# Norms of token tiles 4 to 7 written behind the turns of tiles 2 and 3, and the last product's weight difference written one product sooner

## The chip, the cores and the metric

One core of one Trainium2 chip runs the whole kernel. The metric is the device time of one execution in microseconds (us). Engines are named as in the profile: PE (TensorE matmul), PEld (its weight load), DVE (VectorE), ACT (ScalarE), POOL (GpSimd), SP (SyncE, which issues nearly all DMAs here).

## The reference

An encoder layer over 1024 tokens of width 1024, all in f32. In short:

```python
x = LN1(ALPHA * x + 0.5 * swiglu(x, ffn1_w1, ffn1_w3, ffn1_w2))     # width 2816 inside
...                                                                 # latent attention and S5 scan, merged
x = LN2(ALPHA * x + merged @ w_out)
x = LN3(ALPHA * x + 0.5 * swiglu(x, ffn2_w1, ffn2_w3, ffn2_w2))
x = LN4(ALPHA * x + sigmoid(x @ w_gate) * (p @ w_proj))
```

The change touches the two places where a SwiGLU ends in its layer norm (LN1 and LN3) and the next matmuls begin: the projection `w_u` of the S5 branch after LN1, the gate `ple_w_gate` after LN3.

## The kernel before, in words

**Precision.** Every f32 operand is split in two fp32r parts, high and low (`split`, L62: a copy on ACT, L64, and a subtraction on DVE, L65), and each product is three matmuls: high by high, high by low, low by high.

**The second layers** (`ffn_down`, L353) multiply the hidden activations by `w2` with Strassen's scheme (Winograd's form): seven products of half-sized blocks in the order 1, 5, 6, 3, 7, 2, 4, each over 11 slabs of the inner dimension, taken in six steps `q` (five pairs of slabs and a single one). Products alternate between two sets of four PSUM banks (`pd` and `pdy`). The weight blocks b11, b12, b21, b22 are fetched to SBUF and combined in place on DVE: `less` (L414) lists the products that take a difference, and L429 subtracts, step by step, just ahead of the splits of that step. Product 4, the last one, takes b21 - b11, written into b11's room. Its results complete token tiles 4 to 7 (128 tokens by 1024); tiles 0 to 3 are complete after product 2. `ffn_down` is a generator: it yields the tiles 0 to 3 with their row sums between the steps of product 4, and the tiles 4 to 7 one by one as their last addition (`add`, L392) is written.

**The norms** (`norm_in`, L187) consume these tiles. For each tile `layer_norm` (L113) is written: the mean on DVE (L120), the squares with a running sum on ACT (L123, into a scratch tile `scr`), a square root on ACT (L125), five small DVE operations (L126 to L130) and two passes over the tile on DVE (L133, L135). A normed tile is then *turned*: `transpose_in` (L139) has PE transpose it by eight 128x128 matmuls into a PSUM tile `tln` (L148), which is split into the transposed activations `xhi` (ACT, L64) and `xlo` (DVE, L65). The list `ready` holds normed tiles: with `lag=2` tile 0 is turned after norm 2 is written, tile 1 after norm 3, tile 2 after norm 4, tile 3 after norm 5. Tiles 4 to 7 are turned by `finish` (late turns, in half tiles), which the caller writes after the first half of the next matmuls.

**What follows.** After LN1: four splits of the `w_u` weights (`whi`, `wlo`), then `up` for tokens 0 to 511 (`pu`, 96 matmuls, whose moving operand is one row block of the transposed tiles 0 to 3, so all four must be turned), then `finish`, then `up` for tokens 512 to 1023. The S5 branch's parameters are loaded behind that. After LN3: `pgate` and `pproj` tile by tile (a gate tile j needs only turned tile j), each evacuated by a sigmoid on ACT (L1057, tile `gs`) and two DVE operations (L1058, L1061); `finish` is written between gate tile 3 and gate tile 4. There `scr` and `gs` are tiles of one tag with two buffers, and the transposed activations, the parameters of LN3 and those of LN4 are tiles of another tag (`x` of the pool `fb`) with three.

**The order on each engine** is not the order of writing. The kernel is built by a scheduler that reckons when each instruction's operands will be there; among those that it takes to be ready, the one written earlier goes first, and when none of the early ones is ready, a later one goes. Buffers of a tag are handed out as they are first written in that order. The engine then runs its list strictly in order. The caller's two lines are

```python
finish = norm_in(chain([first], dn), acc, *ln, x1T, fp, spill, 2)          # after LN1; spill stores a turned tile to DRAM
finish = norm_in(chain([first], dn), acc, gt, bt, x3T, fp, lag=2)          # after LN3
```

and LN2 uses the same function with `blocks=True`.

Of the kernel before, what the change touches and what calls it, by code (L numbers as in the profile page):

```python
# [45 lines left out]
def layer_kernel(ctx, tc, A):  # L46
# [68 lines left out]
    def layer_norm(a, sums, gt, bt, pool, out=None):  # L115

        nm, sq, v, y, rs = [sml.tile([128, 1], F32, tag=f"ln{i}", name=f"ln{i}") for i in range(5)]
        V.tensor_scalar(out=nm, in0=sums[:, 0:1], scalar1=sums[:, 1:2], scalar2=-1.0 / D,  # L120
                        op0=ALU.add, op1=ALU.mult)
        scratch = pool.tile([128, 1024], BF16, tag="s", bufs=2, name="scr")
        S.activation(scratch, a, AF.Square, bias=nm, accum_out=sq)  # L123
        V.tensor_scalar(out=v, in0=sq, scalar1=1.0 / D, scalar2=LN_EPS, op0=ALU.mult, op1=ALU.add)
        S.activation(sq, v, AF.Sqrt)  # L125
        V.reciprocal(y, sq)  # L126
        V.tensor_tensor(out=sq, in0=y, in1=y, op=ALU.mult)
        V.tensor_tensor(out=sq, in0=sq, in1=v, op=ALU.mult)
        V.tensor_scalar(out=sq, in0=sq, scalar1=-0.5, scalar2=1.5, op0=ALU.mult, op1=ALU.add)
        V.tensor_tensor(out=rs, in0=y, in1=sq, op=ALU.mult)  # L130
        cs = [slice(0, 1024)] if out is None else [slice(c, c + 512) for c in (0, 512)]
        for c in cs:
            V.scalar_tensor_tensor(out=a[:, c], in0=a[:, c], scalar=nm, in1=gt[:, c], op0=ALU.add, op1=ALU.mult)  # L133
        for c in cs:
            V.scalar_tensor_tensor(out=a[:, c], in0=a[:, c], scalar=rs, in1=bt[:, c], op0=ALU.mult, op1=ALU.add)  # L135
            if out is not None:
                nc.sync.dma_start(out[:, c], a[:, c])
# [49 lines left out]
    def norm_in(steps, acc, gt, bt, xT, pool, done=None, lag=3, blocks=False):  # L187


        ready = []  # L190

        def bring(late):
            j = ready.pop(0)
            if blocks:
                transpose_blocks(acc, j, xT)
            else:
                transpose_in(acc[j], j, xT, late)
            if done:
                done(j)

        def finish(n=8):
            while ready and n:
                bring(True)
                n -= 1

        for j, sums in steps:
            with ExitStack() as after:
                for i in behind_splits:
                    after.enter_context(tc.issue_after(i.ins))
                layer_norm(acc[j], sums, gt, bt, pool)  # L210
            ready.append(j)
            if len(ready) > lag and ready[0] < 4:
                bring(False)
        return finish
# [138 lines left out]
    def ffn_down(fp, acc, x0, hd, w2, homes, hs):  # L353

        W, ends = {}, {}
        sums = [sml.tile([128, 2], F32, tag="sums", bufs=8, name="sums") for _ in range(8)]

        def block(i, q):
            p, n = DUOS[q]
            t, o = (W[i], p) if p < 8 else (ends[i[0]], 3 * i[1] + p - 8)
            return t[:, o:o + n, :]

        def fetch(i):
            if i[0] not in ends:
                ends[i[0]] = homes["end", i[0]]("w2e", F32)
            W[i] = homes[i]("w2w", F32)
            for q in range(len(DUOS)):  # L370
                p, n = DUOS[q]
                behind(lambda: nc.sync.dma_start(block(i, q), w2[i[0], i[1]][:, p:p + n, :]))

        def behind(load):
            if hs:
                with tc.issue_after(hs[-1].ins):
                    load()
            else:
                load()

        X = [pdn.tile([128, 512], F32, tag="dn", name="pd") for _ in range(4)]
        follows = {1: 5, 5: 6, 6: 3, 3: 7, 7: 2, 2: 4}
        ahead = None

        def hload(i, q):
            n = DUOS[q][1] * 512
            return load_raw(hd[i - 1][q].rearrange("p a b -> p (a b)")[:, 0:n], n, hs)

        def add(out, j, n, ps, first, last):
            a = acc[j][:, n * 512:n * 512 + 512]  # L390
            if first or last:
                V.scalar_tensor_tensor(out=a, in0=a, scalar=ALPHA if first else 1.0, in1=ps, op0=ALU.mult, op1=ALU.add,  # L392
                                       accum_out=sums[j][:, n:n + 1] if last else None)
            else:
                V.tensor_tensor(out=a, in0=a, in1=ps, op=ALU.add)

        b11, b12, b21, b22 = (0, 0), (0, 1), (1, 0), (1, 1)

        stages = ((1, 0, True, [(0, 0, True, False)]), (5, 1, True, [(4, 1, True, False)]),
                  (6, 0, False, [(0, 1, True, False)]), (3, 1, False, [(0, 1, False, True)]),  # L400
                  (7, 0, False, [(4, 1, False, True)]), (2, 1, True, [(0, 0, False, True)]),
                  (4, 0, False, [(4, 0, True, True)]))
        want = {1: b11, 5: b12, 6: b22, 2: b21}
        right = {1: b11, 5: b11, 6: b11, 3: b22, 7: b12, 2: b21, 4: b11}
        less = {5: (b12, b11), 6: (b22, b11), 7: (b22, b12), 4: (b21, b11)}
        for i, bank, fresh, reads in stages:
            if i == 1:
                fetch(want[i])
            if bank == 1 and fresh:
                yy = [pup.tile([128, 1024], F32, tag="up", name="pdy") for _ in range(2)]  # L410
                Y = [t[:, c:c + 512] for t in yy for c in (0, 512)]
            P = Y if bank else X
            held = []
            for q, (p, n) in enumerate(DUOS):  # L414
                if q == 0:
                    h = ahead or hload(i, 0)
                else:
                    h = hload(i, q)
                if q == len(DUOS) - 1 and i != 4:
                    ahead = hload(follows[i], 0)  # L420
                if q == 2 and i != 4 and follows[i] in want:
                    fetch(want[follows[i]])
                if q == 4 and i in (1, 5):
                    for j in range(4):
                        behind(lambda: nc.sync.dma_start(acc[j + (i == 5) * 4], x0[j + (i == 5) * 4]))
                w = block(right[i], q)
                if i in less:
                    x, y = (block(b, q) for b in less[i])
                    V.tensor_tensor(out=w, in0=x, in1=y, op=ALU.subtract)  # L429
                hh, hl = [wts.tile([128, 1024], F32R, tag=t, name=o) for t, o in (("uh", "hh"), ("ul", "hl"))]  # L430
                wh, wl = [fp.tile([128, 1024], F32R, tag="v", bufs=4, name=o) for o in ("wh", "wl")]
                split(h[:, 0:n * 512], hh[:, 0:n * 512], hl[:, 0:n * 512])
                last = split(w, *[t[:, 0:n * 512].rearrange("p (a b) -> p a b", a=n) for t in (wh, wl)])
                held.append((p, n, hh, hl, wh, wl))
                if i == 4 and 0 < q < 5:
                    behind_splits[:] = last
                    yield q - 1, sums[q - 1]
                    behind_splits.clear()
                if i == 4 and q == 4:
                    continue  # L440

                def part(t, first_p=held[0][0]):
                    for p, n, hh, hl, wh, wl in held:
                        for a in range(n):
                            ts = slice(a * 512 + t * 128, a * 512 + t * 128 + 128)
                            ws = slice(a * 512, a * 512 + 512)
                            for m, (x, y) in enumerate(((hh, wh), (hh, wl), (hl, wh))):
                                PE.matmul(P[t], lhsT=x[:, ts], rhs=y[:, ws], start=(fresh and p + a == 0 and m == 0),  # L448
                                          stop=(p + a == NP - 1 and m == 2), skip_group_check=True)

                for t in range(4):
                    part(t)
                    if q == len(DUOS) - 1:
                        for j, nn, first, last in reads:
                            add(None, j + t, nn, P[t], first, last)
                        if i == 4:
                            yield 4 + t, sums[4 + t]
                held = []
# [1056 lines left out]
```

## Time and profile before

| | |
|---|---|
| median of 3 runs | 2328.61 us (2328.49 to 2328.64) |
| the profiled execution, its own time | 2328.71 us |
| its span, first to last instruction | 2326.8 us |
| mean granted TensorE clock, as a share of full speed | 0.992 |
| busy: PE, DVE, ACT, POOL | 2260.3, 1543.6, 971.1, 233.9 us |

The profile is one execution. The span leaves out 1.9 us of its own time. PE is busy nearly throughout, so the time is to be found in the few places where PE waits or runs at the lower of its two clock levels. A line of a timeline gives start, duration, engine, line, operation, what it writes and reads, and in brackets the idle time before it and what ended that. Durations of neighbours on one engine overlap a little; the step from one start to the next is what an instruction costs its engine.

### The profile page before, as it was taken

To read this page: it belongs to the slowest core of one execution; us is meant where nothing else is said; L and a number is where in the kernel's file an instruction comes from. 1 tells how busy PE (TensorE), PEld (TensorE's weight loads), DVE (VectorE), ACT (ScalarE), POOL (GpSimd) and SP (SyncE) were. 2 spreads that over 40 slices of the span, in tenths; PEclk is the share of its full clock that TensorE was granted. 3 is DMA by queue.
4 is the path that set the end of the run, shared out by engine and by line. 5 is a ranking of instruction groups with operands and counts; after the bars stand their busy time and mean duration, and the time that the engine had idled before them with its cause. 6 is when DMAs were issued, how large, how long until landed. Compare 5 with 4: busy or idle time off the path is not lost.

```text
span 2326.8 us, 28503 instructions
## 1 busy us (share of the span) xinstructions
PE 2260.3 (97%) x10784; PEld 1863.0 (80%) x10784; DVE 1543.6 (66%) x2437; ACT 971.1 (42%) x1419; POOL 233.9 (10%) x318
## 2 busy tenths in 40 slices
PE   9999999999989899989999999999999999999998
PEld 7888888877777788877888887788888888877776
DVE  7555555676565798947688885585655555755856
ACT  5333333333342344444478772234333333333626
POOL 0000000000003500002255452100000000000000
PEclk9999999999999999999999999999999999999999
DMA  4323333834244232326200115122323235633401
GB/s 158 113 87 118 96 108 97 305 137 157 92 146 146 82 109 85 103 84 256 72 10 19 37 73 218 36 100 77 118 91 114 91 122 196 243 138 112 140 10 73
DMA packets 104474, 265.63 MB, mean 114 GB/s; under 512 B 13328, under 2 KB 27920, under 8 KB 104336
## 3 DMA queue, kind: packets, MB, share of 16 engines
q1 hardware_dynamic: 104336, 263.80, 33.4%
q8 instruction: 85, 1.39, 0.2%
q14 instruction: 53, 0.43, 0.1%
HBM read 189.33 MB, written 74.42 MB: 113 GB/s over the span
## 4 chain that ended last, share of the span: by engine, by line
PE 47%; DVE 5%; ACT 2%; issue 1%; DMA 1%; SPq 0%; POOL 0%; DVEq 0%; ACTq 0%; POOLq 0%
PE px L240 9%; PE py L240 5%; PE pdy L448 4%; PE pd L86 4%; PE pd L448 3%; PE pgate L86 3%; PE ps L86 3%; PE pz L240 2%; PE pov L753 2%; PE tpp L740 2%; PE pya L86 2%; PE pyb L86 2%; PE pq L86 1%; PE pg L86 1%; PE pu L278 1%
## 5 line engine op out<-in xcount | busy, mean ns | idle before, releaser
L64 ACT ACTIVATE whi<-raw 128x1024 fp32r<-128x1024 f32 (+4 forms) x116 | 112.2, 974 | 189.6 <-PE pg L86 99.0
L65 DVE TENSOR_TENSOR wlo<-raw,whi 128x1024 fp32r<-128x1024 f32 (+4 forms) x116 | 137.7, 1192 | 62.8 <-ACT whi L64 60.4
L448 PE MATMUL pd<-wl,hh 128*128 128x512 f32 x352 | 139.6, 398 | 3.1 <-DVE wl L65 3.1
L86 PE MATMUL pg<-xlo,whi 128*128 128x512 f32 x352 | 138.8, 394 | 0.0
L86 PE MATMUL pg<-xhi,whi 128*128 128x512 f32 x352 | 138.7, 394 | 0.0
L448 PE MATMUL pd<-wh,hl 128*128 128x512 f32 x352 | 138.5, 394 | 0.0
L86 PE MATMUL pg<-xhi,wlo 128*128 128x512 f32 x352 | 138.3, 393 | 0.0
L64 ACT ACTIVATE wh<-w2w 128x1024 fp32r<-128x1024 f32 x56 | 59.3, 1059 | 174.3 <-PE pd L448 92.3
L448 PE MATMUL pd<-wh,hh 128*128 128x512 f32 x352 | 120.3, 397 | 1.3 <-ACT wh L64 1.3
L240 PE MATMUL py<-tch,fhl 128*128 128x512 f32 x320 | 106.0, 392 | 0.0
L448 PE MATMUL pdy<-wl,hh 128*128 128x512 f32 x264 | 104.4, 396 | 0.8 <-DVE wl L65 0.8
L448 PE MATMUL pdy<-wh,hl 128*128 128x512 f32 x264 | 104.2, 395 | 0.0
L65 DVE TENSOR_TENSOR hl<-raw,hh 128x1024 fp32r<-128x1024 f32 x84 | 94.6, 1132 | 9.1 <-ACT hh L64 9.1
L64 ACT ACTIVATE fhl<-raw 128x512 fp32r<-128x512 f32 x40 | 25.3, 633 | 179.9 <-PE px L240 177.3
L448 PE MATMUL pdy<-wh,hh 128*128 128x512 f32 x264 | 99.1, 395 | 0.0
L240 PE MATMUL px<-td,thi 128*128 128x512 f32 x320 | 98.8, 390 | 0.0
L65 DVE TENSOR_TENSOR pt<-tpp,pt 128x512 fp32r<-128x512 f32 x128 | 85.6, 685 | 11.6 <-ACT pt L64 10.3
L65 DVE TENSOR_TENSOR wl<-w2w,wh 128x1024 fp32r<-128x1024 f32 x56 | 68.5, 1223 | 33.8 <-ACT wh L64 33.8
L254 DVE TENSOR_TENSOR c<-raw 128x512 f32<-128x512 f32 x40 | 27.6, 689 | 93.9 <-PE px L240 93.9
L727 POOL TENSOR_SCALAR P<-P,sm 128x1024 f32<-128x1024 f32 x64 | 74.7, 1168 | 117.0 <-DVE sm L726 99.3
L86 PE MATMUL ps<-k,qh 96*128 96x512 f32 (+1 forms) x256 | 84.2, 407 | 1.9 <-ACT P L725 1.7
L448 PEld LDWEIGHTS pd<-wl,hh 128*128 128x128 f32 x352 | 66.2, 188 | 21.6 <-DVE wl L65 6.4
(433 smaller groups left out, 6274.1 us busy)
## 6 DMA issues: line engine op xcount, KB each, us to landing
raw<-in_ffn_w_dram SPq DMA_DIRECT2D x86, 512.0 KB, 3.7
raw<-hd SPq DMA_DIRECT2D x70, 512.0 KB, 3.3
hd<-c SPq DMA_DIRECT2D x88, 256.0 KB, 3.4
w2w<-in_ffn_w_dram SPq DMA_DIRECT2D x32, 512.0 KB, 6.4
hd<-s SPq DMA_DIRECT2D x60, 256.0 KB, 3.2
rawx<-in_xT_dram SPq DMA_DIRECT2D x16, 256.0 KB, 6.4
w2e<-in_ffn_w_dram SPq DMA_DIRECT2D x8, 512.0 KB, 8.0
acc<-in_x_dram SPq DMA_DIRECT2D x8, 512.0 KB, 6.2
```

The costliest lines, as they stand in the source:

```text
L64: a = S.activation(hi, src, AF.Copy)
L65: return a, V.tensor_tensor(out=lo, in0=src, in1=hi.bitcast(F32), op=ALU.subtract)
L86: PE.matmul(out, lhsT=a, rhs=b, start=(n == 0), stop=(n == last))
L240: PE.matmul(out, lhsT=x[:, ks], rhs=y[:, k, :], start=(first and n == 0), stop=(n == 11), skip_group_check=True)
L254: V.tensor_tensor(out=c[:, r], in0=r2[:, l], in1=r2[:, r], op=ALU.add)
L278: PE.matmul(o, lhsT=x[:, ks], rhs=b[y][:, k, :], start=(i == 0 and k == 0 and m == 0), stop=(i == 1 and k == 3 and m == 2), skip_group_che ...
L448: PE.matmul(P[t], lhsT=x[:, ts], rhs=y[:, ws], start=(fresh and p + a == 0 and m == 0), stop=(p + a == NP - 1 and m == 2), skip_group_chec ...
L727: G.tensor_scalar(out=P, in0=P, scalar1=sm, scalar2=1.0, op0=ALU.mult, op1=ALU.mult)
L740: PE.transpose(tp[:, k * 128:k * 128 + 128], P[:, (q * 4 + k) * 128:(q * 4 + k) * 128 + 128], idt)
L753: PE.matmul(p[:, 0:256], lhsT=vt[:, k, c0:c0 + 128], rhs=pt[k // 4][b][:, k % 4, :], start=(k == 0 and b == 0), stop=(k == 7 and b == 1))
```

## The change

Two edits. In `ffn_down` product 4 leaves the list `less`, and its subtraction is written in product 2 instead, step by step, behind the splits of b21. The operands, the result and its place are the same. In `norm_in`, when it isn't the form for LN2 (`blocks`), the tiles 4 to 7 are not normed as they come: they go to a list `left`, and if a normed tile waits to be turned, it is turned then (tile 2 when tile 4 comes, tile 3 when tile 5 comes, as before). Their norms are written in `finish`, all four ahead of the late turns.

```diff
-        ready = []
+        ready, left = [], []
...
         def finish(n=8):
+            while left:
+                j, sums = left.pop(0)
+                layer_norm(acc[j], sums, gt, bt, pool)
+                ready.append(j)
             while ready and n:
                 bring(True)
                 n -= 1
 
         for j, sums in steps:
+            if j > 3 and not blocks:
+                left.append((j, sums))
+                if ready:
+                    bring(False)
+                continue
             with ExitStack() as after:
...
-        less = {5: (b12, b11), 6: (b22, b11), 7: (b22, b12), 4: (b21, b11)}
+        less = {5: (b12, b11), 6: (b22, b11), 7: (b22, b12)}
...
                 held.append((p, n, hh, hl, wh, wl))
+                if i == 2:
+                    V.tensor_tensor(out=block(b11, q), in0=w, in1=block(b11, q), op=ALU.subtract)
```

## Rows read from the trace of the kernel before

**Rows 1.** The page's first part: busy time, share of span, instructions.

```profile
PE 2260.3 (97%) x10784; PEld 1863.0 (80%) x10784; DVE 1543.6 (66%) x2437; ACT 971.1 (42%) x1419; POOL 233.9 (10%) x318
```

**Rows 2.** Waits of PE: us in total, times, longest.

```profile
PE pu L86 <- DVE ln L124: 7.5, 2, 6.0
```

**Rows 3.** Stretches behind product 4, first SwiGLU: length, engines' busy time (instructions), clock, DMA.

```profile
663.90:672.10 8.20, 0.76 (x1) 0.29 (x1) 8.20 (x13) 6.83 (x12) 0.00 (x0) 0.68 0.64 205
672.10:677.00 4.90, 4.86 (x11) 3.80 (x12) 4.90 (x25) 0.41 (x2) 0.00 (x0) 0.50 0.05 20
677.00:696.30 19.30, 19.30 (x85) 15.81 (x84) 3.71 (x5) 1.09 (x2) 0.00 (x0) 1.00 0.34 137
```

**Rows 4.** Timeline of PE in that place.

```profile
661.99 1.91 PE L148 MATMUL tln<-idt,acc 128*128 128x128 f32 x16
669.85 0.76 PE L86 MATMUL pu<-xhi,whi 128*128 128x512 f32 x1 [5.95 <-DVE ln L124]
672.14 0.79 PE L86 MATMUL pu<-xlo,whi 128*128 128x512 f32 x1 [1.53 <-DVE ln L124]
```

**Rows 5.** Timeline of DVE in that place.

```profile
663.57 1.22 DVE L65 TENSOR_TENSOR wlo<-raw,whi 128x1024 fp32r<-128x1024 f32 x1
...
664.89 1.28 DVE L133 SCALAR_TENSOR_TENSOR acc<-acc,ln,ln 128x1024 f32<-128x1024 f32 x1
...
668.48 1.22 DVE L65 TENSOR_TENSOR xlo<-tln,xhi 128x1024 fp32r<-128x1024 f32 x1
...
669.67 1.28 DVE L133 SCALAR_TENSOR_TENSOR acc<-acc,ln,ln 128x1024 f32<-128x1024 f32 x1
670.87 1.22 DVE L65 TENSOR_TENSOR xlo<-tln,xhi 128x1024 fp32r<-128x1024 f32 x1
...
698.16 4.88 DVE L65 TENSOR_TENSOR xlo<-tln,xhi 128x512 fp32r<-128x512 f32 x8 [17.45 <-ACT xhi L64]
```

**Rows 6.** Timeline of ACT in that place.

```profile
662.22 1.13 ACT L123 ACTIVATE scr<-acc,ln 128x1024 bf16<-128x1024 f32 x1
...
663.35 1.99 ACT L64 ACTIVATE whi<-raw 128x1024 fp32r<-128x1024 f32 x2
665.25 1.00 ACT L64 ACTIVATE xhi<-tln 128x1024 fp32r<-128x1024 f32 x1
666.15 1.14 ACT L123 ACTIVATE scr<-acc,ln 128x1024 bf16<-128x1024 f32 x1
...
667.28 1.00 ACT L64 ACTIVATE xhi<-tln 128x1024 fp32r<-128x1024 f32 x1
```

**Rows 7.** Timeline of DVE: differences of product 4, during product 3.

```profile
554.17 1.22 DVE L429 TENSOR_TENSOR w2w<-w2w 128x1024 f32<-128x1024 f32 x1
...
562.19 1.82 DVE L429 TENSOR_TENSOR w2e<-w2e 128x1024 f32<-128x1024 f32 x2
```

**Rows 8.** Timeline of SP: first S5 parameter.

```profile
725.34 0.42 SPq L1095 DMA_DIRECT2D c_re<-in_c_re_dram  x1
```

**Rows 9.** Timeline of PE, second SwiGLU: late turns.

```profile
2226.00 1.91 PE L148 MATMUL tln<-idt,acc 128*128 128x128 f32 x16
```

**Rows 10.** Timeline of DVE in that place.

```profile
2215.71 4.88 DVE L135 SCALAR_TENSOR_TENSOR acc<-acc,ln,ln 128x1024 f32<-128x1024 f32 x4
...
2227.61 0.69 DVE L65 TENSOR_TENSOR xlo<-tln,xhi 128x512 fp32r<-128x512 f32 x1
```

**Rows 11.** Timeline of ACT in that place.

```profile
2210.72 0.30 ACT L125 ACTIVATE ln<-ln 128x1 f32<-128x1 f32 x2
...
2224.80 0.60 ACT L1057 ACTIVATE gs<-pgate 128x512 f32<-128x512 f32 x1 [6.35 <-PE pgate L86]
```

**Rows 12.** Groups of ACT, 2190 to 2232: line, tile, count, busy us, mean ns, idle before.

```profile
L1057 ACT ACT_TABLE_LOAD x2 | 2.6, 1283 | 0.9 <-PE pgate L86 0.9
...
L125 ACT ACT_TABLE_LOAD x1 | 1.3, 1283 | 0.0
```

**Rows 13.** Timeline of SP: parameters of LN4.

```profile
2185.33 0.43 SPq L112 DMA_DIRECT2D ln<-in_ln_g_dram  x1
```

## The prediction

> **What bounds the kernel now.** I read the page's busy times first, then the waits of PE, then the stretches and timelines around the wait that the change aims at. PE is busy for 97% of the span [rows 1], so only places where PE waits, or runs at the lower clock level, can give time back. One of its longest waits lies behind the first SwiGLU's product 4: 7.5 us in two pieces, before matmuls of `pu` [rows 2]. The view names a DVE instruction of the norm as releaser, but that is only the last count of a semaphore; the timelines say what PE waited for. PE ends the turns of tiles 2 and 3 at 661.99 + 1.91 = 663.90 and starts `pu` at 669.85, just after the `xlo` of tile 2 (668.48, about 1.2 long) has emptied the PSUM tile that `pu` writes; its second matmul, at 672.14, comes just after the `xlo` of tile 3 (670.87, about 1.2 to 672.1) [rows 4, 5]. In that stretch of 8.2 us DVE is busy all the time with 13 instructions, ACT for 6.83 us [rows 3]. So DVE's list sets when PE goes on. Two of its entries there are first passes over tiles that nobody needs yet: L133 at 664.89 (tile 4) and at 669.67 (tile 5), both ahead of the `xlo` of tile 3 [rows 5]; on ACT the squares of tiles 4 and 5 stand at 662.22 and 666.15, ahead of the `xhi` of tiles 2 and 3 [rows 6]. After the wait PE's granted clock is 0.50, the 1.2 GHz level, until 677.0: 11 matmuls take 4.9 us, where 85 later ones take 19.30, or 0.227 each, at full clock [rows 3]. That costs 4.9 - 11 x 0.227 = 2.4 us more.
>
> **The subtractions written sooner: 0.** The six subtractions of product 4 don't run in product 4. They run from 554.17 to 564.0, during product 3, two products before the place where they are now written and three before their own [rows 7]. Operands and results stay the same, so they can't run sooner than their operands, and nothing about them is on PE's path. If that cover went, their 6.7 us (four of 1.22 and a pair of 1.82) would stand in product 4; the edit moves them the other way. The two SwiGLUs are built alike; I take nothing in either.
>
> **The norms behind the turns, first SwiGLU: -1.8.** The trace does not show the new list, so I bound it. A first pass L133 costs DVE 670.87 - 669.67 = 1.20 us [rows 5], a square costs ACT 667.28 - 666.15 = 1.13 [rows 6]. If both passes leave the place ahead of the last `xlo`, that one ends 2.4 us sooner, if one does, 1.2. The edit does not guarantee either. It makes the norms the last choice, but an engine whose early work is not ready yet takes them all the same. On ACT the square of tile 4 starts at 662.22, before the turns end at 663.90, and ACT has to fill this time with something: two `whi` splits [rows 6] and probably that square again. Then `xhi` of tile 2 starts at 665.25 as before, but `xhi` of tile 3 follows at once, at 666.2 and no longer at 667.28. On DVE three `wlo` splits of 1.2 from 663.57 reach 667.2, the two `xlo` then 669.6 if no L133 slips in and 670.8 if one does, against 672.1. I take the middle of 1.2 and 2.4, 1.8 us; the ends kept are 0 (both slip in) and what the second rival gives. PE still idles from 663.90 to about 668, so the clock falls as before, since it had fallen by half within the 8.2 us (0.68 on average) [rows 3]: 0 from the clock, with 2.4 as the other end.
>
> **What the moved norms cost where they go: 0.** DVE's work in this place stays the same, only its order changes, and DVE has no gap there. So the four norms end about when they end today, 698.16 - 17.45 = 680.7, where DVE runs out of work [rows 5]. PE works through `pu` until 696.3 [rows 3] and only then turns tiles 4 to 7: 15.6 us of cover, and without it the late turns would start late by what is missing. On SP the stores of the normed tiles follow their norms, nothing on PE's path waits for them, and the norms issue no other DMA. The rest of the kernel follows: the S5 parameters are asked for on SP at 725.34 [rows 8], behind `pu`, so what is won at 672 shifts what comes after and is not taken back at once.
>
> **Second SwiGLU: 0.** There the gate tiles need one turned tile each, so PE has work and waits little. The norms of tiles 4 to 7 are now written behind gate tiles 0 to 3. They have slack: their last passes end at 2215.71 + 4.88 = 2220.59, the late turns start at 2226.00 and the first late `xlo` at 2227.61 [rows 9, 10]. Queued behind a norm that is late would be the late turns on PE, and behind these everything. I take 0, since DVE has the same work in that stretch and runs whatever is ready; a loss is the third rival.
>
> **Sum.** 2328.71 (the span of 2326.8 and 1.9 outside it) - 1.8 = 2326.9; the median of the runs lies 0.1 below the profiled execution, so 2326.8.
>
> **Rivals.** (1) *The edit does not change the order that matters.* Both passes slip in ahead of the `xlo` of tile 3 as they do today, because the turns are ready too late. For it: both engines are nearly full there, and the subtractions [rows 7] show that readiness beats the order of writing. Against it: at 669.67 a pass of tile 5 went ahead of the last `xlo` although its `xhi` had ended, 667.28 + 1.0 [rows 6], and by writing order that choice would now fall the other way. It gives 2328.6.
>
> (2) *The turns go straight through.* If neither norms nor the last `wlo` splits stand ahead, the `xhi` of tile 3 runs from 663.90, about 1.0, its `xlo` 1.2 behind it, to 666.1: 6.0 us sooner than 672.1. PE then idles for about 2 us and may keep its clock: 2.4 more. It gives 2328.6 - 8.4 = 2320.2. Against it: the weight splits are ready before the turns and fill both engines.
>
> (3) *The norms of the second SwiGLU come too late, and the kernel gets slower.* ACT runs its list in order. If the scheduler puts the square roots of tiles 4 to 7 behind the sigmoid of gate tile 3 (written earlier now), they start after 2224.80 + 0.60 = 2225.4 and a table load of 1.28, at 2226.7. From there to the end of the last pass it takes between 4.88, the four last passes alone, and 9.9 as today (2210.72 to 2220.59, with other work in between) [rows 10, 11]; the middle is 7.4. The first late `xlo` would wait until 2234.1 instead of 2227.61: 6.5 us, and 2.4 of low clock after that gap. Less the 1.8 won it gives 2328.6 + 8.9 - 1.8 = 2335.7. It decides once the last norm ends after 2227.6, 7 us later than now. For it: the late `xlo` may need the buffer that holds LN3's parameters, so one late norm holds up all. Against it: the squares and roots are ready long before that sigmoid; and buffers are handed out by use, not by writing: LN4's parameters, written behind both `xlo` tiles of that tag, were asked for at 2185.33 [rows 13], so the squares need not wait for the `gs` tiles.
>
> The table load in this place is 1.28 us, taken when a square root and a sigmoid alternate, three times today [rows 12]; four roots alternating with four sigmoids would make eight, 5 x 1.28 = 6.4 us more on ACT, and the last norm would end at 2227.0, still inside the bound above. The Trainium skill, "ScalarE: Activation LUTs", section "Rules for kernel authors", says to group functions by table set and finish one set before the other, which speaks against writing these roots behind sigmoids; it budgets about 2.7 us for a switch. By that figure five more would be an estimated 13.5 us and the last norm would end at 2234.1, as in rival 3, whose chance it shares.
>
> **How the numbers follow.** Forecast 0.55 (2325.0 to 2328.6), rival 1 0.17, rival 2 0.15, rival 3 0.13. 0.2%, about what a measurement of this kernel can tell from no change, is 4.7 us: the forecast and rival 1 lie within it (0.72), rival 2 is faster by more (0.15), rival 3 slower by more (0.13). The range takes in rival 2, 2320.0, and reaches at the upper end half way from the forecast's 2328.6 to rival 3, since two of the four norms may be late and two not: 2332.0.
>
> **What would show it.** In the changed profile: subtractions still during product 3; the last full-tile `xlo` of the first SwiGLU ending 1.2 to 2.4 us sooner relative to the end of the turns (8.2 us now), with at most one L133 ahead of it; the 0.50 clock still there; norms of tiles 4 to 7 done before the late turns in both places. A distance under 5 us, or a clock that stays up, would prove it wrong in favour of rival 2; a wait of PE over 3 us at the second SwiGLU's late turns, in favour of rival 3.

## The result, and the profile after

The changed kernel takes 2339.81 us (median of 5 runs, 2338.47 to 2340.83) against 2328.61 for the kernel before (5 runs, 2327.90 to 2329.31): a ratio of 1.0050, 95% interval 1.0040 to 1.0061. It is 11.2 us slower; the prediction was 2326.8, and its range ended at 2332.0. The profiled execution has a span of 2338.0 us and a mean clock of 0.990.

The page's busy times:

```profile
PE 2262.2 (97%) x10784; PEld 1866.3 (80%) x10784; DVE 1544.8 (66%) x2437; ACT 972.3 (42%) x1419; POOL 234.2 (10%) x318
```

The waits of PE (us in total, times, longest):

```profile
PE tln L148 <- DVE ln L130: 9.2, 1, 9.2
PE pu L86 <- DVE ln L124: 7.5, 2, 5.9
```

The work is the same as before [rows 1]. The wait at `pu` that the change aimed at has not moved [rows 2], and a new one of 9.2 us stands ahead of turns. The rest is a matter of two places.

**The first SwiGLU's tail** is as it was. Its stretches, cut at the same instructions as before [rows 3] (length, busy time of PE, PEld, DVE, ACT, POOL with instructions, clock, DMA share, GB/s):

```profile
662.98:671.18 8.20, 0.77 (x1) 0.29 (x1) 8.20 (x13) 6.84 (x13) 0.00 (x0) 0.68 0.67 213
671.18:676.10 4.92, 4.88 (x12) 3.82 (x13) 4.92 (x26) 0.41 (x2) 0.00 (x0) 0.50 0.02 7
```

The timeline of DVE inside the first of them, to set beside [rows 5]:

```profile
663.91 1.22 DVE L65 TENSOR_TENSOR wlo<-raw,whi 128x1024 fp32r<-128x1024 f32 x1
...
665.22 1.28 DVE L133 SCALAR_TENSOR_TENSOR acc<-acc,ln,ln 128x1024 f32<-128x1024 f32 x1
666.41 1.23 DVE L65 TENSOR_TENSOR wlo<-raw,whi 128x1024 fp32r<-128x1024 f32 x1
667.55 1.23 DVE L65 TENSOR_TENSOR xlo<-tln,xhi 128x1024 fp32r<-128x1024 f32 x1
...
668.74 1.29 DVE L133 SCALAR_TENSOR_TENSOR acc<-acc,ln,ln 128x1024 f32<-128x1024 f32 x1
669.93 1.23 DVE L65 TENSOR_TENSOR xlo<-tln,xhi 128x1024 fp32r<-128x1024 f32 x1
```

One `wlo` has changed places with the L133 of tile 4, and that is all (the two `wlo` that rows 5 leaves out stood behind that L133, at 666.21): both first passes still stand ahead of the last `xlo`. Everything here runs about 0.9 us earlier than before (the turns at 661.07 instead of 661.99), an offset of which half is there at 105 us already and all of it at 603, ahead of this place; the distances here are the same.

**The second SwiGLU's tail** has the loss. The timeline there, of ACT, then of DVE, then of PE (start, duration, and in brackets the idle time before an instruction):

```profile
2199.22 1.28 ACT L1068 ACT_TABLE_LOAD   x1
2206.59 0.60 ACT L1068 ACTIVATE gs<-pgate 128x512 f32<-128x512 f32 x1 [6.09 <-PE pgate L86]
...
2216.97 0.60 ACT L1068 ACTIVATE gs<-pgate 128x512 f32<-128x512 f32 x1 [5.44 <-PE pgate L86]
2223.92 0.60 ACT L1068 ACTIVATE gs<-pgate 128x512 f32<-128x512 f32 x1 [6.35 <-PE pgate L86]
2224.42 1.14 ACT L123 ACTIVATE scr<-acc,ln 128x1024 bf16<-128x1024 f32 x1
...
2200.52 0.21 DVE L120 TENSOR_SCALAR ln<-sums 128x1 f32<-128x1 f32 x1
...
2233.11 1.28 DVE L135 SCALAR_TENSOR_TENSOR acc<-acc,ln,ln 128x1024 f32<-128x1024 f32 x1
...
2234.57 3.67 DVE L135 SCALAR_TENSOR_TENSOR acc<-acc,ln,ln 128x1024 f32<-128x1024 f32 x3
...
2195.00 1.03 PE L148 MATMUL tln<-idt,acc 128*128 128x128 f32 x8
...
2234.53 3.65 PE L148 MATMUL tln<-idt,acc 128*128 128x128 f32 x16 [9.25 <-DVE ln L130]
2240.04 3.37 PE L148 MATMUL tln<-idt,acc 128*128 128x128 f32 x16 [1.86 <-DVE xlo L65]
2243.16 0.48 PE L86 MATMUL pgate<-whi,xhi 128*128 128x512 f32 x1
```

The timeline of PE in the kernel before, ahead of and behind the line in [rows 9]:

```profile
2195.90 1.04 PE L148 MATMUL tln<-idt,acc 128*128 128x128 f32 x8
...
2228.35 0.66 PE L148 MATMUL tln<-idt,acc 128*128 128x128 f32 x4 [0.44 <-DVE xlo L65]
2230.09 1.85 PE L148 MATMUL tln<-idt,acc 128*128 128x128 f32 x12 [1.09 <-DVE xlo L65]
2231.89 0.50 PE L86 MATMUL pgate<-whi,xhi 128*128 128x512 f32 x1
```

The last mean that the squares need is there at 2200.7 (L120), and ACT then idles for 6.09, 5.44 and 6.35 us. Yet the first square runs at 2224.42, right behind the sigmoid of gate tile 3. From there to the end of the last pass, 2234.57 + 3.67 = 2238.24, it takes 13.8 us. PE's late turns wait for the pass over tile 4 (2233.11 + 1.28 = 2234.39) and then run at half speed: 16 turns in 3.65 us, where they took 1.91 before [rows 9]. The stretches of the wait and of the late turns show a clock of 0.53 in the second:

```profile
2225.20:2234.50 9.30, 0.09 (x1) 0.00 (x0) 8.78 (x31) 5.83 (x13) 0.00 (x0) 0.72 0.00 1
2234.50:2243.50 9.00, 7.11 (x34) 6.70 (x35) 8.66 (x13) 4.80 (x8) 0.00 (x0) 0.53 0.20 58
```

The sum closes, by the timelines of PE in both kernels. From tile 2's turn to the first late turn it takes 2234.53 - 2195.00 = 39.53 us, against 2226.00 - 2195.90 = 30.10 before: 9.4 more. From there to the first `pgate` behind the late turns it takes 2243.16 - 2234.53 = 8.63 us against 2231.89 - 2226.00 = 5.89: 2.7 more. Of these 0.3 are a longer wait between the turns (1.86 against 0.44 and 1.09), and 2.4 are the low clock. Together 12.2; less the 0.9 that the profiled run was ahead, 11.3, beside 11.2 between the spans (2338.0 - 2326.8).

### The profile page after: what moved, and what is told of

Same layout as the page of the kernel before. It is cut to its first block, busy times and chain, and to the rows that moved or that the text cites. A ratio compares the mean times of both kernels' runs of the same rounds, so it can differ in the third digit from the quotient of the medians.

```text
span 2338.0 us, 28500 instructions
## 1 busy us (share of the span) xinstructions
PE 2262.2 (97%) x10784; PEld 1866.3 (80%) x10784; DVE 1544.8 (66%) x2437; ACT 972.3 (42%) x1419; POOL 234.2 (10%) x318
## 4 chain that ended last, share of the span: by engine, by line
PE 47%; DVE 5%; ACT 2%; issue 1%; DMA 1%; POOL 0%; SPq 0%; DVEq 0%; ACTq 0%; POOLq 0%
PE px L249 9%; PE py L249 5%; PE pdy L459 4%; PE pd L459 4%; PE pd L86 3%; PE pgate L86 3%; PE ps L86 3%; PE pz L249 2%; PE pov L764 2%; PE tpp L751 2%; PE pya L86 2%; PE pyb L86 2%; PE pq L86 1%; PE pg L86 1%; PE pg L287 1%
```

## The experiments

Two questions were open: what holds the squares behind the last sigmoid in the second SwiGLU, and what it takes to win anything in the first one. Ratios are to the kernel before, run on the same chip (medians 2327.2 to 2328.1), with 95% intervals. The last two versions ran on another chip than the rest.

### Where the loss sits: each part alone

The first edit without the second (the subtraction as in the change, `norm_in` as before):

> The first edit alone: product 4's subtraction written in product 2, the norms as before. If it moves nothing that matters: the subtractions run within 2 us of where they ran (554 to 564) and the time is the one of before, ratio 0.999 to 1.001. If it takes part in the loss or in a gain: outside of that.

Measured: 2327.28 us, ratio 0.9998 (0.9990 to 1.0007). The subtractions run where they ran (first and last start over both SwiGLUs; 554.17 and 2092.6 before):

```profile
L436 DVE TENSOR_TENSOR w2w<-w2w x8: 1217/1222/1226, 554.3 to 2090.8; 128x1024 f32<-128x1024 f32 x8
```

Both edits, but with the norms put back in one SwiGLU only:

```diff
-    def norm_in(steps, acc, gt, bt, xT, pool, done=None, lag=3, blocks=False):
+    def norm_in(steps, acc, gt, bt, xT, pool, done=None, lag=3, blocks=False, defer=True):
...
-            if j > 3 and not blocks:
+            if j > 3 and defer and not blocks:
...
-    finish = norm_in(chain([first], dn), acc, gt, bt, x3T, fp, lag=2)
+    finish = norm_in(chain([first], dn), acc, gt, bt, x3T, fp, lag=2, defer=False)
```

This is the version that defers in the first SwiGLU; the other has `defer=False` at the first call.

> Both edits, but the norms of tiles 4 to 7 are put back only in the first SwiGLU; the second one is written as before. If the whole loss of 11.2 us comes from the second SwiGLU (buffers or order there): 2328.6 us, between 2327 and 2329.5, and the squares of the second SwiGLU back at about 2200 to 2204.5. If the first SwiGLU takes part in the loss: 2333 or more.

> Both edits, but the norms are put back only in the second SwiGLU. If the loss lies there alone: 2339.8 us, between 2338 and 2341.5, and PE's wait of about 9 us ahead of the late turns is there. If the first SwiGLU makes the loss: 2328.6.

Measured: first alone 2328.90, ratio 1.0004 (0.9995 to 1.0013); second alone 2341.24, ratio 1.0056 (1.0043 to 1.0068), with the same 9.2 us wait. So the first edit and the first SwiGLU give and cost nothing that can be measured, and the whole loss is the second SwiGLU's.

### What holds the squares back

The whole change, but the squares of tiles 4 to 7 there write to a scratch tile of their own tag (one buffer, which is the room that was left):

```diff
+            layer_norm(acc[j], sums, gt, bt, pool, tag=own)     # in finish; own="s2" after LN3, else "s"
...
-        scratch = pool.tile([128, 1024], BF16, tag="s", bufs=2, name="scr")
+        scratch = pool.tile([128, 1024], BF16, tag=tag, bufs=2 if tag == "s" else 1, name="scr")
```

> The whole change, but in the second SwiGLU the scratch tile of the squares of tiles 4 to 7 has a buffer of its own and shares none with the gs tiles. Buffer theory (a square written behind gate tile 3 gets the buffer of gs 2 and can't be placed ahead of it): the squares go back to about 2199 to 2206, PE's wait ahead of the late turns falls from 9.25 to below 1 us, and the time is 2328.6, between 2327 and 2330. Order theory (being written behind the sigmoids alone puts them there): the squares stay behind the sigmoid of gate tile 3 at about 2224.4 and the time stays 2339.8. The buffer theory is also wrong if the squares go back but the wait stays.

Measured: 2327.87, ratio 1.0001 (0.9992 to 1.0010). ACT, then PE, in its timeline:

```profile
2199.52 1.14 ACT L123 ACTIVATE scr<-acc,ln 128x1024 bf16<-128x1024 f32 x1
...
2207.50 0.60 ACT L1068 ACTIVATE gs<-pgate 128x512 f32<-128x512 f32 x1
...
2225.55 1.91 PE L148 MATMUL tln<-idt,acc 128*128 128x128 f32 x16
```

The four squares stand ahead of the first sigmoid again, though they are still written behind four of them, and the late turns start without a wait. What they share with `gs` is what held them: the order theory falls, and the whole loss goes with one buffer. Whether a third buffer under the shared tag would have done as much was not tried.

Next the dose: the buffers shared as in the change, the norms written ahead of gate tile 2 or 3 rather than 4 (the late turns stay where they are).

```diff
-        def finish(n=8):
-            while left:
+        def finish(n=8, norms=8):
+            while left and norms:
+                norms -= 1
...
+            if n == 0 and j == 2:      # the other version: 3
+                finish(0)
             if n == 0 and j == 4:
                 finish()
```

> The whole change, but the norms of tiles 4 to 7 are written ahead of gate tile 2 (second SwiGLU), the late turns where they were. Buffer theory: the first square then waits for gs 0 and the second for gs 1, they start at about 2209 and 2213, all squares are through by 2217, no wait of PE over 1 us ahead of the late turns, and the time is that of before, ratio 0.999 to 1.001. If being written behind any sigmoid puts the norms at the end: 2335 or more.

> As the run before, but written ahead of gate tile 3. Buffer theory: the first square waits for gs 1 (about 2213), the second for gs 2 (about 2219.5), so the late turns start 0 to 4 us late: a ratio between 1.000 and 1.003, between the run before and the change. If only being ahead of the last sigmoid counts: as the run before. If buffers don't count: 1.005 as the change.

Measured: ahead of gate tile 2, 2330.98, ratio 1.0012 (1.0004 to 1.0021); ahead of tile 3, 2335.79, ratio 1.0035 (1.0021 to 1.0049); the change, ahead of tile 4, 1.0050. Both expectations were too low (0.999 to 1.001, and 1.000 to 1.003), though the upper end of each lies within the interval. Their mechanism failed in the traces: PE waits 1.91 us where less than 1 was expected, and at tile 3 the first square starts at 2216.08, not at about 2213. The timeline of ACT, then DVE, then PE, with the norms ahead of gate tile 2:

```profile
2212.37 0.59 ACT L1071 ACTIVATE gs<-pgate 128x512 f32<-128x512 f32 x1
2212.85 1.15 ACT L123 ACTIVATE scr<-acc,ln 128x1024 bf16<-128x1024 f32 x1
...
2225.61 3.67 DVE L135 SCALAR_TENSOR_TENSOR acc<-acc,ln,ln 128x1024 f32<-128x1024 f32 x3
2229.19 0.68 DVE L1072 TENSOR_TENSOR gs<-gs,pproj 128x512 f32<-128x512 f32 x1
...
2229.93 1.72 PE L148 MATMUL tln<-idt,acc 128*128 128x128 f32 x8 [1.91 <-DVE gs L1072]
```

and ahead of gate tile 3 (ACT, DVE, PE):

```profile
2215.59 0.60 ACT L1071 ACTIVATE gs<-pgate 128x512 f32<-128x512 f32 x1 [5.44 <-PE pgate L86]
2216.08 1.14 ACT L123 ACTIVATE scr<-acc,ln 128x1024 bf16<-128x1024 f32 x1
...
2211.55 0.69 DVE L1075 SCALAR_TENSOR_TENSOR acc<-acc,gs 128x512 f32<-128x512 f32 x1
...
2226.01 0.17 DVE L126 RECIPROCAL ln<-ln 128x1 f32<-128x1 f32 x1 [1.88 <-ACT ln L125]
...
2229.38 3.65 PE L148 MATMUL tln<-idt,acc 128*128 128x128 f32 x16 [5.48 <-DVE ln L130]
```

In all three versions the first square starts 0.5 us after the start of the last sigmoid written ahead of it (2212.85, 2216.08, 2224.42), even where an older `gs` buffer had been free for long: with the norms ahead of gate tile 3, gate tile 1's was done at 2211.55 + 0.69 = 2212.24 and ACT idled for 5.44 us. So on the chip the square does not wait for a release, as both expectations had it; it stands behind that sigmoid in ACT's list. One reading fits all three versions: a tile's turn for a buffer of the tag does not come before the tiles written ahead of it have theirs. It is not shown, since the list is made by reckoned times that no trace has. By what rule exactly the buffers are handed out is not settled: LN4's parameters did go ahead of tiles written earlier [rows 13].

Ahead of gate tile 2 the squares are early enough for the first turns to start without a wait, and something else is late: three last passes of the norms (to 2229.28) stand on DVE ahead of gate tile 3's multiplication, whose end frees the PSUM that the next turns write. PE idles 1.91 us there and its clock falls after it. In both versions the last square root also stands behind a sigmoid that has a table load on either side, and DVE idles until this root is there: 0.83 us with the norms ahead of gate tile 2, 1.88 with them ahead of tile 3, each time ahead of all four last passes.

### What it takes to win the first SwiGLU's wait

Here the deferral is kept in the first SwiGLU alone, and the norms of tiles 4 to 7 are really held: their instructions on ACT and DVE are ordered behind the two splits of tile 3's turn.

```diff
-                transpose_in(acc[j], j, xT, late)
+                turns[:] = transpose_in(acc[j], j, xT, late)     # now returns its two splits
...
-                layer_norm(acc[j], sums, gt, bt, pool)           # in finish
+                with ExitStack() as after:
+                    for i in turns:
+                        after.enter_context(tc.issue_after(i.ins))
+                    layer_norm(acc[j], sums, gt, bt, pool)
```

> As the first run (norms put back in the first SwiGLU alone), but the norms of tiles 4 to 7 are really held on ACT and DVE behind the two splits of tile 3's turn. If the two first passes and the squares are what makes these splits late: the last full-tile xlo ends 2.4 us sooner after the end of the turns (5.8 us after it, not 8.1) or up to 6 us sooner if ACT's squares counted too, and the time is 2322 to 2326.5. If the turns and the weight splits set it: 2328.6. If the held norms come too late for the late turns: a wait of PE behind pu and more than 2329.

Measured: 2325.31, ratio 0.9988 (0.9979 to 0.9997), the first version that is faster, by 2.8 us. The timeline of DVE, then PE:

```profile
662.95 3.49 DVE L65 TENSOR_TENSOR wlo<-raw,whi 128x1024 fp32r<-128x1024 f32 x3
666.36 2.34 DVE L65 TENSOR_TENSOR xlo<-tln,xhi 128x1024 fp32r<-128x1024 f32 x2
...
668.75 0.79 PE L86 MATMUL pu<-xlo,whi 128*128 128x512 f32 x1 [0.27 <-DVE xlo L65]
```

Its stretches from the end of the turns on:

```profile
663.52:668.75 5.23, 0.76 (x1) 0.29 (x1) 5.23 (x7) 2.13 (x3) 0.00 (x0) 0.72 0.73 233
668.75:673.00 4.25, 4.25 (x11) 3.36 (x12) 3.31 (x10) 4.15 (x8) 0.00 (x0) 0.54 0.30 119
```

No L133 stands ahead of an `xlo` now. From the end of the turns to PE's second `pu` it takes 5.23 us instead of 8.20, 3.0 less; the clock still falls (0.54). What is left is the three `wlo`, 3.49 us. The next version holds these too, behind the `xlo` of tile 3:

```diff
-        us = [wload(A["w_u"][m]) if m < 3 else wload(A["w_u"][m], "v", fp, 4) for m in range(4)]
+        us = [wload(A["w_u"][0])]
+        with tc.issue_after(turns[1].ins):
+            us += [wload(A["w_u"][m]) if m < 3 else wload(A["w_u"][m], "v", fp, 4) for m in range(1, 4)]
```

> The version with the norms held in the first SwiGLU, and three of the four weight splits on DVE (wlo) held too, behind the xlo of tile 3. If what is left of the wait (4.2 + 0.27 us) is these splits: the last full-tile xlo ends 3.6 us after the end of the turns, not 5.2, which is 1.6 us more, about 2323.7; if PE's clock then stays at its upper level, another 2 us, about 2321.5. If the splits that were held come too late for the second pu: a new wait of PE among the pu matmuls and 2325 or more.

Measured: 2321.31, ratio 0.9973 (0.9962 to 0.9984), 6.3 us faster than before. The timeline of PE:

```profile
662.21 1.91 PE L148 MATMUL tln<-idt,acc 128*128 128x128 f32 x16
...
667.79 0.50 PE L86 MATMUL pu<-xlo,whi 128*128 128x512 f32 x1 [0.57 <-DVE xlo L65]
```

Its stretches:

```profile
664.12:667.79 3.67, 0.48 (x2) 0.19 (x2) 2.41 (x3) 2.13 (x3) 0.00 (x0) 1.00 0.11 42
667.79:677.00 9.21, 9.21 (x40) 7.61 (x41) 8.26 (x16) 5.12 (x12) 0.00 (x0) 1.00 0.52 171
```

The distance is 3.67 us, as expected, and in this execution the clock stays at 1.00: 40 matmuls in 9.21 us. (In an execution of the mended version it falls behind the same distance; see the last section.) No new wait appears among the `pu`. Then the weight splits alone, with the norms in the order of before:

> The norms in the order of before in both SwiGLUs; only the three weight splits on DVE (wlo) of the first one are held behind the xlo of tile 3. If the weight splits are as much of the wait as the first passes are: DVE has then both xlo tiles where the xhi allow, with two L133 between, the last xlo ends 5.9 us after the end of the turns (8.2 before), and the time falls by 2.3 us, a ratio of about 0.999. If holding the norms is what counts and the splits alone give nothing: ratio 1.000 within 0.0005. If the splits alone give all that the run with both gave: 0.9973.

Measured: 2325.18, ratio 0.9990 (0.9981 to 0.9998). The timeline of PE:

```profile
661.86 1.91 PE L148 MATMUL tln<-idt,acc 128*128 128x128 f32 x16
...
669.81 0.80 PE L86 MATMUL pu<-xlo,whi 128*128 128x512 f32 x1 [0.81 <-DVE xlo L65]
```

The second `pu` comes 669.81 - 663.77 = 6.0 us after the turns. Norms and weight splits are worth about the same, 2.8 and 2.3 us by the ratios; together they give 6.3 (3.7 to 8.8), and the intervals do not tell whether that is more than the sum. Of these three profiled executions only the one with both held keeps its clock up.

### The change with its faults mended

Norms put back in both SwiGLUs; held with the weight splits in the first one; own scratch buffer in the second one.

> The whole change with what the runs so far found at fault mended: norms put back in both SwiGLUs, held together with three wlo splits behind tile 3's turn in the first one, and a scratch buffer of their own in the second one. If the order of writing in the second SwiGLU costs and gives nothing once the buffer is there: 0.9973 as the version that defers in the first alone, 0.9962 to 0.9984. If deferring in the second one gives something by itself: below 0.996. If it costs something: above 0.9985.

Measured: 2322.78, ratio 0.9978 (0.9969 to 0.9987), within what was expected if the order of writing there costs and gives nothing. The late turns of the second SwiGLU start without a wait, as before [rows 9]. Deferring in the second SwiGLU is worth nothing that shows beside the version that defers in the first alone, which beats both kernels with the smaller edit.

## Why the prediction was wrong, point by point

**Second SwiGLU: 0.** This is the step that failed. It said that DVE "has the same work in that stretch and runs whatever is ready", and rival 3 that "the squares need not wait for the `gs` tiles", because LN4's parameters had gone ahead of tiles written earlier [rows 13]. The squares were ready and ACT was idle; the tag that they share with `gs` kept them behind all four sigmoids. The run with a buffer of its own shows that this alone is the loss. The term was not 0 but +12.2 by the timelines: 9.4 of waiting ahead of the late turns, and behind their start 2.4 of low clock and 0.3 of longer waits.

**Rival 3** had the right place and side, at a chance of 0.13 and a price of 8.9 less 1.8. Its price took only the square roots as late: from 2226.7, 4.88 to 9.9 us to the last pass. In the trace the squares start the chain, at 2224.42, and it takes 13.8. Its low clock of 2.4 us measured 2.4, though it was priced from other matmuls. It let the late `xlo` wait for the last norm; in the trace PE waits already for the first. The range took only half of this rival in; even its full price, 2335.7, would have left the 2339.8 outside.

**The table loads.** Eight were feared in this place, by the alternation of roots and sigmoids. There were three (2199.22, 2226.94 and one at 2245.07), each 1.28 us, since the norms came in one block; the kernel before has three as well [rows 12]. The rule of the Trainium skill ("ScalarE: Activation LUTs", section "Rules for kernel authors") is to finish one table set before the other. It does not tell these versions apart: the version with the scratch buffer of its own alternates (2206.21, 2208.12 and 2211.51), but it makes three loads too, and it is some 11 us faster because its squares run ahead of the sigmoids. The alternation does cost something where there were five loads, in the versions with the norms ahead of gate tile 2 or 3: the 0.83 and 1.88 us for which DVE idles there. The traces do not bear out the 2.7 us a switch that the prediction takes from that section for its estimate: with the norms ahead of gate tile 2, ACT ends a root at 2219.33, loads, and starts the sigmoid at 2220.64, 1.3 us for the switch.

**First SwiGLU: -1.8.** Wrong, 0: rival 1 took place. The claim was that by writing order the choice at 669.67 "would now fall the other way". It did not: at 668.74 the pass of tile 5 still goes first, although the `xhi` of tile 3 had ended, at 666.36 + 1.01 = 667.37 (timeline of ACT):

```profile
666.36 1.01 ACT L64 ACTIVATE xhi<-tln 128x1024 fp32r<-128x1024 f32 x1
```

An engine's list is fixed when the kernel is built, by reckoned times; what the trace shows as ready at that moment is no evidence of what was reckoned ready. What was reckoned is not on record, so why the list came out so stays open. That the passes lengthen the wait was right: with the norms truly held the wait shrinks by 3.0 us, the 2.4 of the first passes and some 0.6 more.

**The clock: 0** was right for a distance of 5.2 us (0.54 after it) and for 8.2 (0.50). **Rival 2** named the rest: its two conditions were that neither norms nor `wlo` splits stand ahead, it forecast 8.4 us, and the run that meets both gives 6.3 (3.7 to 8.8 by the interval). Of its 6.0 us for the wait 4.5 came (8.20 less 3.67), in the main since it left out the `xhi` of tile 2, about 1 us, which ACT runs ahead of that of tile 3.

**The subtractions: 0** was right, 0.9998. **The cover of the moved norms: 0** was right in the first SwiGLU: with the norms held their last pass ends at 681.35 (677.68 + 3.67), and in the version that wins at 680.12 + 3.67 = 683.79, where the late turns start at 689.64 without a wait. The cover there is 5.9 us instead of 15.6.

## What to carry to other kernels

Before moving a step, list what it takes from a pool, not only what it reads: a scratch tile that shares a tag with tiles of another stage can tie the two stages together in the order of writing, and here a buffer of its own costs 2 KB a partition (1024 elements of bf16) against 11 us. Writing work later does not by itself make an engine do it later; where the order on an engine matters, state it as a dependence, and look at everything that stands ahead of the critical instruction, here three weight splits beside the norms. And price a rival by the whole chain from the first held instruction to the consumer.

## What the runs showed of the hardware that was not expected

How long PE pauses does not alone tell whether its clock falls. In the winning version 3.67 us with two matmuls in them left it at 1.00. The mended version has the same 3.67 us in the same place, and its clock falls 1.26 us later. Its stretches (PEclk is the number after the engines):

```profile
663.77:667.44 3.67, 0.47 (x3) 0.19 (x2) 2.41 (x3) 2.13 (x3) 0.00 (x0) 1.00 0.11 42
668.70:672.08 3.38, 3.38 (x10) 2.61 (x9) 2.57 (x6) 1.14 (x2) 0.00 (x0) 0.51 0.62 196
```

Eight matmuls start in the second of them, 0.42 us apart instead of 0.23, which makes 1.5 us more. So the clock can go either way behind this distance. With one profile of each version it is not shown how often it stays up, nor whether the spread of the winning version's runs (2320.09 to 2325.83) comes from it. With the norms ahead of gate tile 2 the clock fell behind a pause of only 1.91 us; there PE had been turning tiles just before and turned tiles again behind it. The stretches there:

```profile
2228.02:2229.93 1.91, 0.00 (x1) 0.01 (x1) 1.91 (x4) 1.68 (x3) 0.00 (x0) 1.00 0.00 0
2229.93:2232.87 2.94, 1.71 (x8) 1.13 (x8) 2.94 (x6) 1.19 (x2) 0.00 (x0) 0.59 0.15 10
2232.87:2236.00 3.13, 3.13 (x14) 3.03 (x15) 2.92 (x5) 1.72 (x3) 0.00 (x0) 0.50 0.40 158
```

The same place in the kernel before, with pauses of 0.44 and 1.09 us between the turns, stays at 1.00. What it was in the work around the pause that made the difference was not tried. The level 0.50 is the 1.2 GHz one.
